# Keys on both partition halves by transposes in place of a DMA, and a new order of activation functions in a decoder layer

## The chip, the cores and the metric

The kernel runs on one core of a Trainium2 chip. The metric is the device time of one launch in microseconds (us), the median of several runs. Lower is better.

## The reference

The program is one decoder layer on a sequence of 256 tokens with 2048 features, all in float32. The part that matters here is the mixer in the middle: one product of the normalised input with a wide weight `w_in` gives queries, keys, values, the inputs of an RWKV-7 recurrence, and gates.

```python
x = x + 0.5 * swiglu(rms_norm(x, ffn1_norm), ...)
h = rms_norm(x, mix_norm); p = h @ w_in
q, k, v, p_rwkv, gates = split(p)
# 16 query heads of 64, 4 key/value heads, window 128, one sink logit for each head
s = where(valid, q k^T / 8, -1e30); m = max(max(s), sink)
e = exp(s - m); pr = e / (sum(e) + exp(sink - m)); y_attn = pr v
# RWKV-7: decay and rate from small products, then a scan over time
w_log = -softplus(-(w0 + tanh(xw) @ w2)) - 0.5      # decay = exp(-exp(w_log))
a = sigmoid(a0 + xa @ a2);  g = sigmoid(xg) @ g2
x = x + (sigmoid(g1) * (y_attn @ w_proj_attn) + sigmoid(g2) * (y_rwkv @ w_proj_rwkv)) @ w_out
x = x + cross_attention(x, mem); x = x + 0.5 * swiglu(rms_norm(x, ffn2_norm), ...)
return rms_norm(x, final_norm)
```

## The kernel before

TensorE (PE) does all matrix products, and nearly all of its time goes to products with weights that are read once from HBM. To keep float32 accuracy, every weight and every activation is split into a high part and a low part, and each product is three matmuls: high x high (line 412), high x low weight (413), low activation x high (414). ScalarE (ACT) casts a weight tile to its high part (line 339), VectorE (DVE) subtracts it from the raw tile to get the low part (line 340). `product` goes over the rows of a weight in items of two 128-row blocks. In the mixer one item is twelve matmuls: six for each half of the tokens. Two items ahead of the one in use are split in advance, and there are three buffers each for high and low parts.

All other work is written as Python generators ("steps") that are put into groups with `bg.spawn`. `product` calls `bg.tick()` after each half item (six matmuls), and at each tick the generators move on by one `yield`. So the interleaving of small work with products is fixed when the program is built. `idle(n)` lets n ticks pass, and `wait_for(name)` yields until another generator has added the name to `bg.seen`. Within that order a scheduler of the language decides the final order on each engine, and `tc.issue_after(ins)` adds an edge that holds an instruction behind `ins` in its engine's queue.

The edited part is the start of the mixer, in this order of products: queries (two products), keys and values (one), then the 288 "small" columns of RWKV, then RWKV keys (two), gates, and so on.

- Keys and values: `scaled` evicts the product to `tok_kv` with the norm's factor (line 783). `keys_values` transposes the 256 key columns on PE (`feat`, line 600), and two ACT copies (line 810) bring the heads to a layout where head kv stands on one half of the partitions. Scores need a key head on both halves, since two query heads share one matmul tile. So the other half is filled by two DMAs from `kd` to `kd`, issued by GpSimd (POOL, line 811). Two DVE copies (line 814) take the values out of `tok_kv`. Three ticks later "kv" is seen.
- Attention: eight generators `attend(kv, qb)`, at most two of them at a time. Scores are matmuls on 64 partitions into score banks of the ring `mm`, which has three (line 831); DVE evicts them with the mask (837), takes the maximum (844) and the negated maximum (849); ACT takes exponentials (856); DVE normalises (864); PE transposes (870) and ACT copies to `pt` (873); PE multiplies with V (878); ACT and DVE split the result (885, 886).
- Decay and rate: `decay_and_rate` waits for the small columns and for the whole attention, then takes a tanh (939) and a sigmoid (940), two small products (950), sixteen sigmoids (957), a scan on DVE (964), and exponentials (978, 982, 983, 985).
- ACT holds the tables of one set of functions at a time. Where the next function is not in it, an ACT_TABLE_LOAD stands ahead of it. In this part, from the first exponential of attention to the last of the decay, there are seven, at lines 856, 940, 856, 957, 978, 957 and 982.

Of the kernel before, what the change touches and what calls it, by code (L numbers as in the profile page):

```python
# [9 lines left out]
AF = mybir.ActivationFunctionType  # L10
# [5 lines left out]
P = 128  # L16
# [7 lines left out]
DECAY = 0.6065306597126334  # L24
# [108 lines left out]
def decoder_layer(ctx: ExitStack, tc: tile.TileContext, a: dict, out: bass.AP):  # L133
# [9 lines left out]
    bg = Interleave()  # L143
# [24 lines left out]
    def idle(n):  # L168
        for _ in range(n):
            yield  # L170
# [596 lines left out]
    with tc.tile_pool(name="mx", bufs=1, reuse_waits="tile") as sp:  # L767
# [12 lines left out]
        def scaled(pb, r, n=512):  # L780
            s = t4("tok", (P, 2, 512))
            for t in range(2):
                act.activation(s[:, t, :n], pb[t][:, :n], AF.Copy, scale=r[t])
            return s
# [11 lines left out]
        for h in range(2):  # L796
            tok = scaled(product(n2.x, W["w_in"]), n2.r)
            qt.append(t4("qt"))
            bg.spawn("feat", to_features(tok, qt[h], "q"))
        tok_kv = scaled(product(n2.x, W["w_in"]), n2.r)  # L800
        kd = t4("kd")
        vt = t4("vt", (P, 2, KV_W))

        def keys_values():

            b = feat(tok_kv, C4[:2])
            v = kd[:].rearrange("p (c e) t -> p c e t", e=2)
            for e in range(2):
                r, o = slice(64 * e, 64 * e + 64), slice(64 - 64 * e, 128 - 64 * e)
                act.copy(v[r, :, e, :], b[r])  # L810
                pool.dma_start(v[o, :, e, :], v[r, :, e, :])
            yield
            for t in range(2):
                dve.tensor_copy(vt[:, t, :], tok_kv[:, t, KV_W : 2 * KV_W])
            yield from idle(3)
            bg.seen.add("kv")

        bg.spawn("feat", keys_values())
        ya = act_tiles("ya", 2)
        sink4 = sinks[:].rearrange("p (k c e) -> p k e c", k=4, c=2)  # L820

        def attend(kv, qb):
            yield from wait_for("kv")
            w = P * (qb + 1)
            tq = slice(qb * P, qb * P + P)
            s = t4("s", (P, 2, 2, T))
            b = [mm() for _ in range(2)]
            for c in range(2):
                for e in range(2):
                    r = slice(64 * e, 64 * e + 64)  # L830
                    pe.matmul(
                        b[e][:, c * w : (c + 1) * w], qt[kv // 2][r, 2 * (kv % 2) + c, tq],
                        kd[r, kv, :w], start=True, stop=True,
                    )
            bias = abias[:, 1 - qb :, :].rearrange("p a b -> p (a b)")
            for e in range(2):
                dve.scalar_tensor_tensor(
                    s[:, e, :, :w], b[e][:, : 2 * w].rearrange("p (c w) -> p c w", c=2), 0.125,
                    bias.unsqueeze(1).to_broadcast([P, 2, w]), ALU.mult, ALU.add,
                )  # L840
            yield
            s3 = s[:].rearrange("p e c w -> p (e c) w")
            m = stat.tile([P, 4], F32, tag="m", name="m")
            dve.tensor_reduce(m[:], s3[:, :, :w], AX.X, ALU.max)
            sk = sink4[:, kv]
            m22 = m[:].rearrange("p (e c) -> p e c", e=2)
            dve.tensor_tensor(m22, m22, sk, ALU.max)
            nm = stat.tile([P, 4], F32, tag="nm", name="nm")
            dve.tensor_scalar(nm[:], m[:], -1.0, None, ALU.mult)
            es = stat.tile([P, 4], F32, tag="es", name="es")  # L850
            dve.tensor_tensor(es[:].rearrange("p (e c) -> p e c", e=2), sk, m22, ALU.subtract)
            yield
            den = stat.tile([P, 4], F32, tag="den", name="den")
            act.activation(es[:], es[:], AF.Exp)
            for i in range(4):
                act.activation(
                    s3[:, i, :w], s3[:, i, :w], AF.Exp, bias=nm[:, i : i + 1],
                    accum_out=den[:, i : i + 1],
                )
            yield  # L860
            dve.tensor_tensor(den[:], den[:], es[:], ALU.add)
            dve.reciprocal(den[:], den[:])
            for i in range(4):
                dve.tensor_scalar(s3[:, i, :w], s3[:, i, :w], den[:, i : i + 1], None, ALU.mult)
            yield
            pt = t4("pt", (P, 2, 4, P))
            for kb in range(qb + 1):
                b = tr()
                for i in range(4):
                    pe.transpose(  # L870
                        b[:, i * P : (i + 1) * P], s3[:, i, kb * P : (kb + 1) * P], ident[:]
                    )
                act.copy(pt[:, kb], b[:].rearrange("p (i q) -> p i q", i=4))
            yield
            b = tr()
            for kb in range(qb + 1):
                for e in range(2):
                    pe.matmul(
                        b[64 * e : 64 * e + 64, : 2 * P], vt[:, kb, kv * 64 : kv * 64 + 64],
                        pt[:, kb, 2 * e : 2 * e + 2, :].rearrange("p c q -> p (c q)"),  # L880
                        start=kb == 0, stop=kb == qb,
                    )
            b3 = b[:, : 2 * P].rearrange("p (c q) -> p c q", c=2)
            hi, lo = (ya.at(p, 2 * kv, 2)[:, :, tq] for p in range(2))
            act.copy(hi, b3)
            dve.tensor_tensor(lo, b3, f32(hi), ALU.subtract)
            if qb:
                ya.done |= {2 * kv, 2 * kv + 1}
            if kv == 3 and qb:
                bg.seen.add("attn")  # L890
# [42 lines left out]
        def decay_and_rate():  # L933
            yield from wait_for("small")
            yield from wait_for("attn")
            wa = t4("wa", (P, RW))
            pool.dma_start(wa[0:64, :], W["rwkv_w2"])
            pool.dma_start(wa[64:128, :], W["rwkv_a2"])
            act.activation(xwa[0:64, :], xwa[0:64, :], AF.Tanh)
            act.activation(xg, xg, AF.Sigmoid)  # L940
            yield
            for h in range(2):
                cs.append(t4("cs"))
                aa.append(t4("aa"))
                for q in (0, 2):
                    b = [mm() for _ in range(2)]
                    for i in range(2):
                        for e in range(2):
                            r, c = slice(64 * e, 64 * e + 64), (4 * h + q + i) * P
                            pe.matmul(  # L950
                                b[e][:, i * T : (i + 1) * T], wa[r, c : c + P], xwa[r, :],
                                start=True, stop=True,
                            )
                    for i in range(2):
                        for e, (dst, bias) in enumerate(((cs[h], w0), (aa[h], a0))):
                            c = 4 * h + q + i
                            act.activation(
                                dst[:, q + i, :], b[e][:, i * T : (i + 1) * T], AF.Sigmoid,
                                bias=bias[:, c : c + 1],
                            )  # L960
                    yield from idle(2)
            for h in range(2):
                for c in range(4):
                    dve.tensor_tensor_scan(
                        cs[h][:, c, :], keep2, cs[h][:, c, :], 0.0, ALU.mult, ALU.add
                    )
                    if c % 2:
                        yield
                c3 = halves(cs[h])
                mid = stat.tile([P, 8], F32, tag="mid", name="mid")  # L970
                dve.tensor_copy(mid[:], c3[:, :, 63])
                dve.tensor_tensor(
                    c3, c3, mid[:].unsqueeze(2).to_broadcast([P, 8, P]), ALU.subtract
                )
                dec.append(stat.tile([P, 4], F32, tag="dec", name="dec"))
                dve.tensor_tensor(dec[h][:], cs[h][:, :, 127], mid[:, 1:8:2], ALU.add)
                yield
                act.activation(dec[h][:], dec[h][:], AF.Exp, scale=-DECAY)

                ee.append(t4("ee", (P, 8, P)))  # L980
                e0.append(stat.tile([P, 8], F32, tag="e0", name="e0"))
                act.activation(e0[h][:], mid[:], AF.Exp, scale=DECAY)
                act.activation(ee[h][:], c3, AF.Exp, scale=-DECAY)
                yield
                act.activation(cs[h][:], cs[h][:], AF.Exp, scale=DECAY)
                yield
            bg.seen.add("decay")
# [526 lines left out]
```

## Time and profile before

| | us |
|---|---|
| median of three runs | 2266.72 |
| lowest and highest of the three | 2265.14, 2268.05 |
| the profiled execution's own time | 2268.04 |
| its span in the profile | 2266.3 |
| PE busy | 2248.0 (99%) |
| DVE busy | 1781.8 (79%) |
| ACT busy | 1232.0 (54%) |
| POOL busy | 134.0 (6%) |

Times in profile rows count from the start of the span. In rows of a timeline the columns are start, duration, engine, line, operation, and in brackets the idle time of the engine ahead of it and what ended that. In rows of stretches they are the stretch, its length, then the busy time and the number of instructions for each engine, the granted clock of PE (1.00 is full speed), the share of DMA time and GB/s. In rows of waits they are the engine and line that waited, what it waited for, the total, the count and the longest. PE's matmuls are pipelined, so that their durations overlap; the distance of their starts is what one costs.

### The profile page before, as it was taken

The page shows a single profiled execution, that of the slowest core. Times are in us where ns is not written, and L with a number is a line of the kernel's source. Part 1 is how long each engine was busy: PE and PEld are TensorE (multiplying, and loading weights), DVE is VectorE, ACT ScalarE, POOL GpSimd, SP SyncE. Part 2 cuts the span into 40 slices and gives each one's busy share as a digit, 9 for nine tenths or more (in the row PEclk, how much of TensorE's full clock was granted, in tenths as well). Part 3 has the DMA queues.
Part 4 walks back from the last instruction along what each step waited for, and adds up shares of the span by engine and source line. Part 5 has one row for each costly group of instructions (what it writes and reads, how often), then busy time and mean ns, then how long its engine had stood idle before and what let it go on. Part 6 is the DMA issues. An engine that isn't in the chain of part 4 may idle for free.

```text
span 2266.3 us, 28104 instructions
## 1 busy us (share of the span) xinstructions
PE 2248.0 (99%) x10613; PEld 1843.9 (81%) x10613; DVE 1781.8 (79%) x2283; ACT 1232.0 (54%) x1655; POOL 134.0 (6%) x194
## 2 busy tenths in 40 slices
PE   9999999999999999999999999999999999999998
PEld 7888888888888877788888888888888888888886
DVE  7899989998988477895444466547899988998987
ACT  6555555555556477544344446456555455555554
POOL 1000000000001000201220030001000000000001
PEclk9999999999999999999999999999999999999999
DMA  7565565565556544677533576657555566556564
GB/s 262 186 208 200 186 215 193 186 209 200 199 197 198 167 122 140 196 231 211 148 87 90 161 260 223 198 165 269 195 193 203 198 204 204 186 201 208 186 205 147
DMA packets 219239, 432.75 MB, mean 191 GB/s; under 512 B 14139, under 2 KB 16416, under 8 KB 219104
## 3 DMA queue, kind: packets, MB, share of 16 engines
q1 hardware_dynamic: 210432, 404.78, 54.3%
q0 software_dynamic: 8208, 25.39, 3.6%
q8 instruction: 83, 1.36, 0.3%
q10 hardware_dynamic: 464, 0.79, 0.1%
q14 instruction: 52, 0.43, 0.1%
HBM read 417.56 MB, written 13.11 MB: 190 GB/s over the span
## 4 chain that ended last, share of the span: by engine, by line
PE 90%; issue 4%; DVE 3%; DMA 1%; ACT 1%; POOL 0%; SPq 0%; POOLq 0%; DVEq 0%; ACTq 0%
PE acc L412 18%; PE acc L413 18%; PE acc L414 18%; PE mm L413 8%; PE mm L414 8%; PE mm L412 8%; PE tr L600 2%; PE tr L413 2%; PE tr L414 2%; PE tr L412 2%; PE mm L1213 1%; DVE lo L340 1%; PE tr L1182 1%; DVE x L573 0%; DMA raw<-in_w_out_dram 0%
## 5 line engine op out<-in xcount | busy, mean ns | idle before, releaser
L340 DVE TENSOR_TENSOR lo<-raw,hi 128x1024 fp32r<-128x1024 f32 (+1 forms) x770 | 895.6, 1165 | 346.3 <-ACT hi L339 344.4
L339 ACT CAST hi<-raw 128x1024 fp32r<-128x1024 f32 (+1 forms) x770 | 759.7, 997 | 737.2 <-PE acc L414 511.5
L412 PE MATMUL acc<-hi,xhi 128*128 128x512 f32 (+1 forms) x1196 | 477.8, 400 | 1.8 <-ACT xhi L627 1.8
L413 PE MATMUL acc<-lo,xhi 128*128 128x512 f32 (+1 forms) x1196 | 466.5, 390 | 1.6 <-DVE lo L340 1.6
L414 PE MATMUL acc<-hi,xlo 128*128 128x512 f32 (+1 forms) x1196 | 465.6, 390 | 0.0
L412 PEld LDWEIGHTS acc<-hi,xhi 128*128 128x128 f32 x1196 | 225.7, 189 | 51.3 <-issue 5.4
L413 PEld LDWEIGHTS acc<-lo,xhi 128*128 128x128 f32 x1196 | 225.9, 189 | 48.9 <-DVE lo L340 3.4
L414 PEld LDWEIGHTS acc<-hi,xlo 128*128 128x128 f32 x1196 | 225.3, 188 | 47.5 <-DVE xlo L628 1.0
L347 ACT CAST thi<-raw 128x1024 fp32r<-128x1024 f32 x172 | 179.0, 1051 | 62.2 <-DVE raw L368 48.8
L348 DVE TENSOR_TENSOR tlo<-raw,thi 128x1024 fp32r<-128x1024 f32 x172 | 208.5, 1221 | 0.7 <-ACT thi L347 0.4
L412 PE MATMUL mm<-hi,xhi 128*128 128x512 f32 x380 | 149.3, 393 | 0.0
L414 PE MATMUL mm<-hi,xlo 128*128 128x512 f32 x380 | 148.1, 390 | 0.0
L413 PE MATMUL mm<-lo,xhi 128*128 128x512 f32 x380 | 148.1, 390 | 0.0
L413 PE MATMUL acc<-lo,hhi 128*128 128x512 f32 x372 | 145.5, 391 | 0.8 <-DVE lo L340 0.8
L414 PE MATMUL acc<-hi,hlo 128*128 128x512 f32 x372 | 145.5, 391 | 0.0
L412 PE MATMUL acc<-hi,hhi 128*128 128x512 f32 x372 | 144.9, 390 | 0.0
L414 PEld LDWEIGHTS mm<-hi,xlo 128*128 128x128 f32 x380 | 71.3, 188 | 15.0
L412 PEld LDWEIGHTS mm<-hi,xhi 128*128 128x128 f32 x380 | 71.4, 188 | 14.5
L413 PEld LDWEIGHTS mm<-lo,xhi 128*128 128x128 f32 x380 | 71.4, 188 | 14.5
L413 PEld LDWEIGHTS acc<-lo,hhi 128*128 128x128 f32 x372 | 69.8, 188 | 15.5 <-DVE lo L340 1.2
L412 PEld LDWEIGHTS acc<-hi,hhi 128*128 128x128 f32 x372 | 69.8, 188 | 14.4
L414 PEld LDWEIGHTS acc<-hi,hlo 128*128 128x128 f32 x372 | 69.9, 188 | 13.9
(386 smaller groups left out, 3551.6 us busy)
## 6 DMA issues: line engine op xcount, KB each, us to landing
raw<-in_ffn_w_up_dram SPq DMA_DIRECT2D x88, 1024.0 KB, 5.5
raw<-in_ffn_w_down_dram SPq DMA_DIRECT2D x88, 1024.0 KB, 5.2
raw<-in_ffn_w_gate_dram SPq DMA_DIRECT2D x84, 1024.0 KB, 5.2
raw<-in_w_in_dram SPq DMA_DIRECT2D x136, 512.0 KB, 3.8
raw<-in_w_out_dram SPq DMA_DIRECT2D x32, 512.0 KB, 4.5
raw<-in_w_proj_attn_dram SPq DMA_DIRECT2D x16, 512.0 KB, 3.7
raw<-in_w_proj_rwkv_dram SPq DMA_DIRECT2D x16, 512.0 KB, 6.1
raw<-in_w_cross_kv_dram SPq DMA_DIRECT2D x16, 512.0 KB, 4.0
```

Source lines behind the costliest of these rows:

```text
L339: at["hi"] = act.copy(hi[:, s], raw[:, s])
L340: at["lo"] = dve.tensor_tensor(lo[:, s], raw[:, s], f32(hi[:, s]), ALU.subtract)
L347: act.copy(hi[:], v[:])
L348: dve.tensor_tensor(lo[:], v[:], f32(hi[:]), ALU.subtract)
L412: pe.matmul(o, xh, hi, start=first, stop=False, **how)
L413: pe.matmul(o, xh, lo, start=False, stop=False, **how)
L414: pe.matmul(o, xl, hi, start=False, stop=last, **how)
L600: pe.transpose(b[:, o : o + P], tok[:, t, col : col + P], ident[:])
L1182: pe.matmul(b[e][:, m * P : (m + 1) * P], x1[r, j, cs_], x2[r, j, cs_], start=True, stop=True,)
L1213: pe.matmul(vb[:, o : o + P][:, r], lhs(e), rhs[:, r], start=first and e == 0, stop=True, **ek,)
```

## The change

The heads of the keys are evicted twice, side by side: one ACT activation for each half of the tokens reads each 64-column key head two times from PSUM and writes a tile of 512 columns, and a second one evicts the values straight into `vt`. The generator that already serves the queries, `to_features`, then transposes four blocks of 128 columns (eight transposes, two copies) into `kd`, so that each head stands on both halves of the partitions. The DMAs, the DVE copies and the pause of three ticks go. In `attend`, two plain yields become `idle(2)`, and the last exponential is remembered. The tanh and the first sigmoid are held behind that exponential, and the decay's exponentials behind the last of the sixteen sigmoids. In the built program, the table loads in this part are then three, ahead of the first attention exponential, the first sigmoid (940 before) and the first decay exponential (978 before). Numbers of lines after this part are lower by three to four in the changed kernel.

```diff
-        tok_kv = scaled(product(n2.x, W["w_in"]), n2.r)
+
         kd = t4("kd")
         vt = t4("vt", (P, 2, KV_W))
-
-        def keys_values():
-
-            b = feat(tok_kv, C4[:2])
-            v = kd[:].rearrange("p (c e) t -> p c e t", e=2)
-            for e in range(2):
-                r, o = slice(64 * e, 64 * e + 64), slice(64 - 64 * e, 128 - 64 * e)
-                act.copy(v[r, :, e, :], b[r])
-                pool.dma_start(v[o, :, e, :], v[r, :, e, :])
-            yield
-            for t in range(2):
-                dve.tensor_copy(vt[:, t, :], tok_kv[:, t, KV_W : 2 * KV_W])
-            yield from idle(3)
-            bg.seen.add("kv")
-
-        bg.spawn("feat", keys_values())
+        pb = product(n2.x, W["w_in"])
+        tok = t4("tok", (P, 2, 512))
+        for t in range(2):
+            act.activation(
+                tok[:, t, :].rearrange("p (h e d) -> p h e d", h=4, e=2),
+                pb[t][:, :KV_W].rearrange("p (h d) -> p h d", h=4).unsqueeze(2).to_broadcast(
+                    [P, 4, 2, 64]
+                ),
+                AF.Copy, scale=n2.r[t],
+            )
+            act.activation(vt[:, t, :], pb[t][:, KV_W : 2 * KV_W], AF.Copy, scale=n2.r[t])
+        bg.spawn("feat", to_features(tok, kd, "kv"))
...
             for i in range(4):
-                act.activation(
+                at["exp"] = act.activation(
                     s3[:, i, :w], s3[:, i, :w], AF.Exp, bias=nm[:, i : i + 1],
...
                 dve.tensor_scalar(s3[:, i, :w], s3[:, i, :w], den[:, i : i + 1], None, ALU.mult)
-            yield
+            yield from idle(2)
             pt = t4("pt", (P, 2, 4, P))
...
                 act.copy(pt[:, kb], b[:].rearrange("p (i q) -> p i q", i=4))
-            yield
+            yield from idle(2)
             b = tr()
...
-            act.activation(xwa[0:64, :], xwa[0:64, :], AF.Tanh)
-            act.activation(xg, xg, AF.Sigmoid)
+            with tc.issue_after(at["exp"].ins):
+                act.activation(xwa[0:64, :], xwa[0:64, :], AF.Tanh)
+                act.activation(xg, xg, AF.Sigmoid)
...
-                            act.activation(
+                            sigmoid = act.activation(
                                 dst[:, q + i, :], b[e][:, i * T : (i + 1) * T], AF.Sigmoid,
...
-                act.activation(dec[h][:], dec[h][:], AF.Exp, scale=-DECAY)
+                with tc.issue_after(sigmoid.ins):
+                    act.activation(dec[h][:], dec[h][:], AF.Exp, scale=-DECAY)
...
-                act.activation(e0[h][:], mid[:], AF.Exp, scale=DECAY)
-                act.activation(ee[h][:], c3, AF.Exp, scale=-DECAY)
+                with tc.issue_after(sigmoid.ins):
+                    act.activation(e0[h][:], mid[:], AF.Exp, scale=DECAY)
+                    act.activation(ee[h][:], c3, AF.Exp, scale=-DECAY)
```

## The prediction, made before the changed kernel ran

> **What bounds the kernel now.** I read the page's first part, then the waits of TensorE (PE) between 784 and 900 us, where the edited code runs, then stretches of that part.
>
> ```profile
> span 2266.3 us, 28104 instructions
> PE 2248.0 (99%) x10613; PEld 1843.9 (81%) x10613; DVE 1781.8 (79%) x2283; ACT 1232.0 (54%) x1655; POOL 134.0 (6%) x194
> ```
> ```profile
> core 0: us, PE busy (x) PEld busy (x) DVE busy (x) ACT busy (x) POOL busy (x), PEclk, DMA share, GB/s
> 784.00:811.00 27.00, 25.50 (x159) 21.41 (x158) 16.87 (x41) 14.96 (x35) 1.27 (x2) 0.87 0.48 141
> 811.00:823.00 12.00, 10.98 (x63) 7.03 (x61) 8.90 (x27) 8.44 (x27) 0.00 (x0) 1.00 0.30 88
> 823.00:840.00 17.00, 16.72 (x86) 12.01 (x85) 13.61 (x33) 13.27 (x33) 3.81 (x6) 1.00 0.52 141
> 840.00:855.00 15.00, 14.69 (x73) 10.67 (x73) 10.86 (x27) 10.93 (x29) 0.00 (x0) 1.00 0.39 119
> 855.00:875.00 20.00, 17.79 (x85) 12.12 (x84) 14.06 (x21) 17.24 (x31) 3.05 (x4) 1.00 0.20 57
> 875.00:910.00 35.00, 35.00 (x156) 28.21 (x156) 27.38 (x27) 25.21 (x33) 2.28 (x4) 1.00 0.64 194
> ```
>
> PE is busy 2248.0 of 2266.3 us, so this change can only win idle PE or a slow PE clock. The stretches are the first pair of attention blocks (784 to 811), the other three pairs, the decay (855 to 875) and what follows. PE idles 1.50, 1.02, 0.28, 0.31 and 2.21 us in them, 5.32 in all, then nothing: from 875 to 910 it is busy 35.00 of 35.00. The only clock below 1.00 is in the first. Idle PE in these stretches and that slow clock are all there is to win.
>
> ```profile
> PE acc L413 <- DVE lo L340: 1.6, 2, 1.3
> PE mm L831 <- DMA kd<-kd: 1.3, 1, 1.3
> PE mm L950 <- ACT cs L957: 0.9, 1, 0.9
> PE tr L870 <- DVE s L864: 0.7, 2, 0.5
> PE tr L878 <- ACT pt L873: 0.6, 1, 0.6
> ```
>
> Each row has the total, the count and the longest. The change touches the causes of all five.
>
> **Keys without the DMA.** PE reaches the first scores (L831) while the keys' DMA, issued by POOL at 786.59, is under way:
>
> ```profile
> 786.59 1.27 POOL L811 DMA_DIRECT2D kd<-kd  x2 [55.50 <-ACT kd L810]
> 790.61 0.93 PE L831 MATMUL mm<-kd,qt 64*128 64x128 f32 x8 [1.33 <-DMA kd<-kd]
> 791.71 2.07 PE L831 MATMUL mm<-kd,qt 64*128 64x256 f32 x6 [0.17 <-DVE s L837]
> ```
> ```profile
> 788.25:791.66 3.41, 1.96 (x15) 1.20 (x13) 1.33 (x4) 0.53 (x1) 0.00 (x0) 1.00 0.92 251
> 791.66:798.49 6.83, 6.78 (x26) 5.96 (x27) 4.77 (x12) 2.90 (x8) 0.00 (x0) 0.50 0.24 70
> 870.17:873.58 3.41, 2.12 (x10) 1.24 (x8) 3.31 (x5) 3.39 (x5) 0.00 (x0) 1.00 0.15 58
> ```
>
> The wait costs 1.33 us. Then the granted clock is 0.50 for 6.83 us, with PE busy in nearly all of them: 6.83 x 0.5 = 3.4 us of work lost, more than the wait itself. Ahead of the drop PE was busy 1.96 of 3.41 us (57%); I took half of 6.83 as the length to compare. A stretch as long, on the same grid, with 2.12 busy (62%) kept its clock at 870. So I read a threshold near 60% of 3.41 us, crossed here because of the DMA wait. [...]
>
> What replaces the DMA: the built order has four more transposes (eight for four), and the first scores wait for the first of two copies into kd only.
>
> ```profile
> 784.98 0.70 PE L600 MATMUL tr<-ident,tok 128*128 128x128 f32 x4
> 785.43 0.38 PE L412 MATMUL acc<-hi,xhi 128*128 128x288 f32 x1
> 787.24 0.29 PE L413 MATMUL acc<-lo,xhi 128*128 128x288 f32 x1
> 787.37 0.29 PE L414 MATMUL acc<-hi,xlo 128*128 128x288 f32 x1
> 785.71 1.19 ACT L810 COPY kd<-tr 64x512 f32<-64x512 f32 x2
> 786.34 0.49 DVE L814 COPY vt<-tok 128x256 f32<-128x256 f32 x2
> ```
>
> Four transposes hold PE from 784.98 to 785.43: +0.45. Two copies into kd stay two (0.6 each, now all 128 partitions). DVE loses two copies of vt (0.49 together); ACT gains two evictions of 256 columns, 0.5 each by the sigmoid rows below, bounds 0.3 to 0.7. They stand ahead of the first kd copy, which then ends near 786.8. PE needs it at 787.6, since its 288-column items and four transposes lie between. So they cost nothing here; with the cover gone, 0.8 us at most. POOL loses two DMAs, for which nothing else queued.
>
> Scores now start one item (12 matmuls) earlier in PE's order, with less product work between them and the softmax:
>
> ```profile
> 796.25 1.28 ACT L856 ACT_TABLE_LOAD   x1
> 797.54 0.40 ACT L856 ACTIVATE s<-s,nm 128x128 f32<-128x128 f32 x1
> 801.26 0.65 ACT L339 CAST hi<-raw 128x576 fp32r<-128x576 f32 x1
> 800.82 1.57 PE L831 MATMUL mm<-kd,qt 64*128 64x128 f32 x12
> 801.80 1.14 DVE L864 TENSOR_SCALAR s<-s,den 128x256 f32<-128x256 f32 x4
> ```
>
> Before, 7.5 us pass from the end of the scores (791.71 + 2.07 = 793.78) to the end of the exponentials (801.26), and 1.7 more to normalised scores (801.80 + 1.14 = 802.94). PE, at half clock, had work all that time. After: scores near 787.7 to 790.7; exponentials end 7.5 later, at 798.2; normalised at 799.9. PE's work between is 42 short matmuls, 0.13 apart (787.24 and 787.37) = 5.6, then 1.5 of the next scores and 0.5 of transposes: it arrives at 798.4. The cast of the next weights stands behind the exponentials in ACT's order, so it lands at 798.9, and its low half, behind the normalising on DVE, at 800.6. I count +1.2 of new idle: 0.4 for the cast and 0.8 in transposes and low half. Bounds: 0 (if PE arrives later) and 2.0.
>
> First pair: -1.33 - 3.4 + 0.45 + 1.2 = -3.1 us.
>
> **Two pauses for one in the attention steps.** Before the transposes and before the product with V, each pair now lets two half items pass, not one. The 0.6 (pt) and 0.7 (s) waits above should shrink. Against it, the fourth pair issues all its scores in a row with three score banks, so the fourth waits for the first's eviction (0.17 above), and everything behind it. I take 0, bounds -1.6 (all idle from 811 to 855: 1.02 + 0.28 + 0.31) and +1.5 (as much new).
>
> **Fewer table loads.** Seven loads stand in this part before; three remain in the built order, since the sigmoids now follow all the exponentials, and the decay's exponentials follow all sigmoids.
>
> ```profile
> L957 ACT ACTIVATE aa<-mm,rv 128x256 f32<-128x256 f32 x8 | 3.8, 493 | 1.5 <-PE mm L950 1.5
> ```
> ```profile
> 867.39 0.39 PE L412 MATMUL acc<-hi,xhi 128*128 128x512 f32 x1
> 867.62 0.40 PE L413 MATMUL acc<-lo,xhi 128*128 128x512 f32 x1
> 867.67 1.28 ACT L957 ACT_TABLE_LOAD   x1
> 869.34 0.47 ACT L957 ACTIVATE aa<-mm,rv 128x256 f32<-128x256 f32 x1
> 869.70 0.48 ACT L957 ACTIVATE cs<-mm,rv 128x256 f32<-128x256 f32 x1
> 870.41 2.01 ACT L339 CAST hi<-raw 128x1024 fp32r<-128x1024 f32 x2
> 872.28 2.35 DVE L340 TENSOR_TENSOR lo<-raw,hi 128x1024 fp32r<-128x1024 f32 x2
> 873.55 0.50 PE L413 MATMUL acc<-lo,xhi 128*128 128x512 f32 x1 [1.29 <-DVE lo L340]
> ```
>
> Four loads less are 4 x 1.28 = 5.1 us of ACT. That is no PE time except where ACT ends a wait: from 855 to 875, where ACT is busy 17.24 of 20. There loads and sigmoids push a weight cast to 870.41, its low half follows at 872.28, and PE waits 1.29. In the built order one cast now stands behind each four sigmoids, and the groups of decay matmuls (L950) are 12 product matmuls apart, 12 x 0.23 = 2.8 us by the two PE rows' starts. Sigmoids start 0.36 apart (869.34, 869.70) and a cast takes 1.0 (2.01 for two), so ACT needs 4 x 0.36 + 1.0 = 2.4 and keeps up. So the 0.92 wait for a bank (the L950 row above, 0.9) goes too. I take -2.1 of the 2.21 idle, bounds -2.2 and 0. Tanh and sigmoid are held behind the last exponential; behind them ACT has casts and copies for attention's end, and the work waiting for tanh (L950) comes 12 matmuls later, so I cost the wait at 0. Past this, the RWKV chain runs 36 product matmuls later in PE's order and ends 102 ahead of its first user, so 0, bounds -0.5 and +1.
>
> **Sum.** -3.1 + 0 - 2.1 = -5.2 us on the profiled execution, whose own time was 2268.04 us (span plus 1.7): 2262.8. Its time is 1.3 above the median of the three runs, 2266.72. I cannot tell whether the profiled one is slower as such or whether the clock drop comes in some runs only (the three spread from 2265.14 to 2268.05). I take half of it off: 2262.1, which is 0.2% under the median.
>
> **The rivals.**
> [...]
> - *The decay keeps its waits* (0.09): the casts come late behind sigmoids and PE waits for lo as before. Time 2262.1 + 2.1 = 2264.2.
> - *A clean run* (0.10): no idle left from 784 to 875. -5.32 - 3.4 + 0.45 = -8.3, so about 2268.0 - 8.3 - 0.65 = 2259.1.
> - *Slower* (0.07): the half clock comes once in each pair, since each now queues scores, bank wait and softmax wait densely. It decides once PE is busy under about 60% of 3.41 us in each of four pairs, as 57% did once before. Then 4 x 3.4 = 13.6 on top: 2275.7, 0.4% slower than 2266.72.
>
> **How the numbers follow.** My forecast has 0.60, and its own range is 2260 to 2264.5. 0.2% (4.5 us, about what a measurement of this kernel can tell from no change) puts the mark at 2262.2, inside it: I give 0.36 of the 0.60 to faster, 0.24 to within. With the clean run faster is 0.46; with the first two rivals within is 0.47; slower is 0.07. The range leaves out the slower rival and the edges: 2258.6 (the clean run, half a microsecond lower) to 2266.5 (2265.5 and one more for the pairs).
>
> **What would show it.** Right: no slow clock near 790; no DMA into kd; first scores with a wait of 0.5 or less; PE idle from 784 to 811 near 1.2; three table loads; PE idle from 855 to 875 under 0.5. Wrong: a clock of 0.50 anywhere in the attention; PE idle over 2 us in the first or the last pair; a PE wait for lo behind the sigmoids; more than 1 us of idle past 900.

## The result, and the profile after

The changed kernel takes 2262.53 us (median of 16 runs, 2262.00 to 2263.34); the kernel before, run beside it, 2266.15 (median of 16, 2264.81 to 2268.45). The ratio is 0.9985, with a 95% interval from 0.9978 to 0.9992: 3.6 us or 0.15% faster. The forecast was 2262.1, "faster" and "within 0.2%" nearly even. So the time came out as forecast; the experiments show that most of its terms did not.

The head of the page after, and the stretches of the edited part (columns as before):

```profile
span 2261.6 us, 28110 instructions
PE 2246.8 (99%) x10617; PEld 1845.5 (82%) x10617; DVE 1778.4 (79%) x2281; ACT 1226.9 (54%) x1653; POOL 132.2 (6%) x192
```
```profile
784.00:811.00 27.00, 26.84 (x181) 22.17 (x179) 19.87 (x50) 18.78 (x51) 0.00 (x0) 1.00 0.43 133
811.00:823.00 12.00, 10.96 (x60) 6.87 (x59) 7.72 (x24) 8.12 (x26) 1.14 (x2) 1.00 0.26 87
823.00:840.00 17.00, 16.92 (x91) 12.47 (x90) 14.01 (x37) 9.80 (x22) 1.84 (x4) 1.00 0.61 185
840.00:855.00 15.00, 15.00 (x80) 10.62 (x79) 8.75 (x20) 13.75 (x36) 2.00 (x3) 1.00 0.34 107
855.00:875.00 20.00, 20.00 (x97) 15.19 (x96) 15.22 (x22) 15.10 (x28) 0.28 (x2) 1.00 0.43 131
```

PE's idle time is now 0.16, 1.04, 0.08, 0 and 0 us, where it was 1.50, 1.02, 0.28, 0.31 and 2.21. The clock is 1.00 throughout. The waits of PE from 784 to 900 us are down to three:

```profile
PE tr L600 <- ACT tok L783: 0.8, 1, 0.8
PE tr L600 <- DVE yalo L882: 0.3, 1, 0.3
PE mm L827 <- DVE s L833: 0.2, 1, 0.2
```

Three table loads are left, as the built order had said (1.28 us each, as before, where the last six stood at the turns between exponentials and sigmoids, 832.48 to 872.44 us):

```profile
791.99 1.28 ACT L852 ACT_TABLE_LOAD   x1
848.26 1.28 ACT L937 ACT_TABLE_LOAD   x1
868.10 1.28 ACT L976 ACT_TABLE_LOAD   x1
```

The end of the first pair's scores, and the cast that stands behind its exponentials:

```profile
789.15 1.13 PE L827 MATMUL mm<-kd,qt 64*128 64x256 f32 x6 [0.16 <-DVE s L833]
797.00 0.66 ACT L339 CAST hi<-raw 128x576 fp32r<-128x576 f32 x1
```

Stretches cut by the clock hold different work in the two kernels. A fairer cut is by PE's product matmuls (lines 412 to 414), of which both kernels have the same 8958: from the 3301st to the 3421st (first pair), to the 3523rd (other pairs), the 3619th (decay), the 4195th (up to the RWKV chain) and the 4963rd (the chain). The length in each row is then the time of the same product work. First before, then after:

```profile
778.75:810.93 32.18, 30.68 (x181) 25.69 (x180) 18.31 (x43) 17.01 (x38) 1.27 (x2) 0.89 0.47 137
810.93:851.30 40.37, 39.02 (x202) 27.77 (x201) 30.75 (x83) 30.03 (x82) 3.81 (x6) 1.00 0.41 118
851.30:885.83 34.53, 32.05 (x155) 23.07 (x154) 21.64 (x29) 30.37 (x51) 3.05 (x4) 1.00 0.43 124
885.83:1027.64 141.81, 141.50 (x656) 114.42 (x654) 126.19 (x161) 67.79 (x73) 20.46 (x19) 1.00 0.69 211
1027.64:1311.41 283.77, 283.36 (x1665) 235.41 (x1664) 135.93 (x162) 127.13 (x230) 43.41 (x69) 1.00 0.48 137
```
```profile
778.96:807.55 28.59, 28.43 (x186) 23.79 (x184) 18.02 (x42) 17.64 (x40) 0.00 (x0) 1.00 0.41 126
807.55:846.96 39.41, 38.29 (x202) 27.57 (x201) 30.72 (x83) 28.14 (x81) 2.98 (x6) 1.00 0.43 134
846.96:877.78 30.82, 30.82 (x154) 22.45 (x152) 19.22 (x28) 24.00 (x42) 2.28 (x4) 1.00 0.46 143
877.78:1019.81 142.03, 141.27 (x655) 114.21 (x653) 117.83 (x154) 71.05 (x79) 21.05 (x17) 1.00 0.65 206
1019.81:1306.51 286.70, 286.29 (x1665) 238.18 (x1665) 142.16 (x169) 126.74 (x230) 45.09 (x70) 1.00 0.44 138
```

Differences: -3.6, -1.0, -3.7, +0.2 and **+2.9**; with +0.2 ahead and +0.2 behind, the span's -4.7 (the medians stand 3.6 apart). By kind and number the small matmuls in each stretch are the same in both kernels, but for the four more transposes in the first. The last row is the surprise. PE is busy in all but 0.4 us in both, at a clock of 1.00, with 896 small matmul records in both traces, and still needs 2.9 us more.

### The profile page after: what moved, and what is told of

The parts are those of the page before. It is cut to its first block, busy times and chain, and to the rows that moved or that the text cites. A ratio compares the mean times of both kernels' runs of the same rounds, so it can differ in the third digit from the quotient of the medians.

```text
span 2261.6 us, 28110 instructions
## 1 busy us (share of the span) xinstructions
PE 2246.8 (99%) x10617; PEld 1845.5 (82%) x10617; DVE 1778.4 (79%) x2281; ACT 1226.9 (54%) x1653; POOL 132.2 (6%) x192
## 4 chain that ended last, share of the span: by engine, by line
PE 96%; DVE 2%; issue 1%; DMA 1%; ACT 1%; SPq 0%; POOL 0%; POOLq 0%; DVEq 0%; ACTq 0%
PE acc L412 19%; PE acc L413 19%; PE acc L414 19%; PE mm L414 8%; PE mm L412 8%; PE mm L413 8%; PE tr L600 2%; PE tr L413 2%; PE tr L412 2%; PE tr L414 2%; PE mm L1212 1%; PE tr L1181 1%; DVE lo L340 1%; DMA raw<-in_w_out_dram 0%; PE mm L827 0%
```

## The experiments

Each kernel ran beside the kernel before. "Alternating" below is said of the score matmuls of the RWKV chain (line 1182 before, 1181 after): two heads, one on each half of the rows, three matmuls each. The program writes them in turn. In the built order 8 of the 16 blocks keep that order before and 5 after; 6 and 8 have three of one head ahead of three of the other, the rest is mixed. (The expectations below speak of three such blocks in the changed kernel and six with the keys alone; the traces have five and seven, in a few of which the pairs start 13 ns apart and not 6 to 7.) I take it that the scheduler's choice depends on when the score banks come free, which no run tests.

**Keys alone.** The keys' part of the diff on the kernel before, nothing else:

```diff
-        tok_kv = scaled(product(n2.x, W["w_in"]), n2.r)
...
-        bg.spawn("feat", keys_values())
+        pb = product(n2.x, W["w_in"])
...
+        bg.spawn("feat", to_features(tok, kd, "kv"))
```

> The kernel before with the keys' part of the change alone (double eviction, eight transposes, no DMA, no pause of three ticks); the pauses in attention and the order of the functions stay as before. My theory: the DMA wait of 1.33 us was the cause of the half clock, so both go: -1.33 - 3.4 + 0.45 for four more transposes = -4.3 us by the end of the attention; the seven table loads and the 2.2 us of idle from 855 to 875 stay. The RWKV chain stands 12 product matmuls earlier, with 6 of its blocks of score matmuls alternating between the row halves where before has 8, for about +1.3. Sum -3.0 us. Rival: the half clock has another cause and stays: -1.33 + 0.45 + 1.3 = +0.4 us.

Measured: 2265.69 us (2265.39 to 2266.97), ratio 0.9997 (0.9988 to 1.0006): no difference that can be told. No half clock (1.00 from 784 to 811 us) and no DMA wait, as expected, and the first pair takes 29.67 us for 32.18, though 76 small matmuls now fall into this stretch for 60. But the chain's stretch takes 285.49 us, 1.7 more than before, and of the waits near the decay the one for cs grows from 0.9 us, the one for lo stays:

```profile
PE mm L946 <- ACT cs L953: 1.4, 2, 1.1
PE acc L413 <- DVE lo L340: 1.3, 1, 1.3
```

Both theories were off at the median: it stands 0.9 us below the runs beside it, not 3.0 below and not 0.4 above.

**Function order and pauses alone**, with the keys by DMA as before:

```diff
-            yield
+            yield from idle(2)
...
+            with tc.issue_after(at["exp"].ins):
...
+                with tc.issue_after(sigmoid.ins):
```

> The kernel before with the order of the functions and the pauses of two ticks, but the keys by DMA as before. My theory: the 1.33 us wait and the half clock (3.4 us) stay; the decay wins 3.7 us as in the whole change, the later pairs of attention about 1; the RWKV chain stands 48 product matmuls later with 3 alternating blocks of score matmuls for 8, for about +3.5. Sum -1.2 us. Rival: table loads are no time of TensorE at all and the gain near the decay came from the keys: +3.5 us.

Measured: 2271.14 us (2269.40 to 2277.36), ratio 1.0026 (1.0015 to 1.0036). Slower than either theory had it. The wait for the keys' DMA is there, as expected (1.6 us for 1.33); the half clock, also expected, did not come in the profiled execution (1.00 from 784 to 811 us). The decay is without waits, but the work behind it falls late among the products. From 870 to 1030 us PE waits 2.4 us for a cast, 1.2 for a bank of `lt` and 0.5 for a low half; the stretch ahead of the chain takes 147.4 us for 141.8, the chain 288.0.

**Scores two ticks later**, the DMA kept:

```diff
-            yield from idle(3)
+            yield from idle(5)
             bg.seen.add("kv")
```

> The kernel before with the keys' pause five ticks instead of three: the DMA stays, but the first scores come 12 short matmuls (12 x 0.13 = 1.6 us) later, so that it has landed. My theory: the wait alone made the half clock, so 1.33 + 3.4 go, at most 1 us of new idle comes, and the chain's order (6 alternating blocks for 8, 4 half ones for 1) costs 0.7: -3.0 to -4.0 us. Rival: the clock falls for another reason than this wait (the matmuls on half the rows, the DMA traffic): the half clock stays and the time changes by -1.3 + 0.7 = -0.6 us.

Measured: 2261.03 us (2260.36 to 2261.58), ratio 0.9976 (0.9967 to 0.9985): 5.6 us faster, more than the 3 to 4 that my theory had, and the best of all kernels here. One number in the program beats the whole change by 1.5 us. The wait is gone and the clock stays at 1.00; the first pair takes 26.9 us, with 56 small matmuls in the stretch for 60. The decay's wait for lo falls from 1.3 to 0.5 us although all seven table loads are still there. That work, too, moved against the products; I take this to be the reason.

**The chain shifted alone.** Six ticks, 36 product matmuls, ahead of the mark that the decay is done:

```diff
+            yield from idle(6)
             bg.seen.add("decay")
```

> The kernel before with six ticks of pause (36 product matmuls) ahead of the mark that the decay is done, so that the RWKV chain has the place and the order of the changed kernel; nothing else is edited. My theory: attention and decay as before, half clock included; the stretch of the chain takes 3.0 us more for the same matmuls, since 3 of the score blocks alternate between the row halves where before has 8; whole time +3.0 us. Rival: the order of the small matmuls is indifferent and the lost 3 us came from elsewhere in the change: 0 us, within 0.5.

Measured: 2268.68 us (2268.04 to 2271.19), ratio 1.0011 (1.0002 to 1.0020). Three stretches of this kernel: the first pair, 3.41 us with the DMA wait in them, and the chain:

```profile
778.71:808.22 29.51, 27.88 (x182) 23.11 (x181) 17.86 (x43) 17.01 (x38) 1.28 (x2) 1.00 0.49 149
787.24:790.65 3.41, 2.07 (x16) 1.71 (x15) 1.52 (x2) 0.99 (x2) 0.59 (x1) 1.00 0.85 218
1025.11:1311.82 286.71, 286.30 (x1664) 238.06 (x1665) 142.16 (x169) 126.69 (x230) 44.95 (x70) 1.00 0.45 138
```

The chain takes 286.71 us, the changed kernel's 286.70 to a hundredth, and PE's matmuls stand in the same order in both: the shift alone makes the 2.9 us. And something nobody had asked: up to the decay this program has the same order as the kernel before, and waits the same 1.3 us for the DMA, yet in this execution the clock did not fall. The same 120 products took 29.51 us in place of 32.18. So the half clock comes in some executions only, and the 6.83 us of it cost 2.7 us.

**Alternation forced, in the changed kernel:**

```diff
+                one = None
...
-                        pe.matmul(
+                        with tc.issue_after(one.ins) if one else nullcontext():
+                            one = pe.matmul(
```

> The changed kernel, with the six score matmuls of each RWKV block held in the order of the code (each behind the one before), so that they alternate between the two halves of the rows; in the built order 3 blocks alternate wholly as before and 13 are one matmul, a little product work, then five that alternate, in place of 3, 4 and 3 by 3. My theory: the order of the halves sets the time of these matmuls; at 0.87 us for an alternating block and about 1.15 for one and five, 21.6 us of this line become 17.6: -4.0 us against the changed kernel, 2258.5. Rival: the order only shows which bank came free late, and TensorE waits that time out instead: 0, 2262.5.

Measured: 2262.64 us (2262.40 to 2263.21), where the changed kernel has 2262.53: nothing. The chain takes 286.8 us. By the distances of the starts the score matmuls did become cheaper, by 2.0 us, but the first of each block now stands apart, product work is broken into 83 times for 71, and the products around took 1.9 us more. 14 blocks became one and five, 2 alternate wholly. So the edit made a new cost where it took one away; it tells nothing against the alternation, and nothing for it.

**The same edit in the kernel before.**

> The same edit in the kernel before, where 8 blocks alternate already and 8 become one and five. My theory: 19.4 us of this line become 16.2: -3.2 us against before, and the stretch of the RWKV chain is then about 1.4 us shorter than in the changed kernel with the same edit, not 2.9. Rival: waits take the place of the order: 0.

Measured: 2266.51 us (2264.94 to 2268.12), ratio 1.0001 (0.9992 to 1.0010). The chain takes 283.11 us for 283.77. Of the 3.2 us expected 0.7 came. By the starts the score matmuls take 2.2 us less, but product work takes 1.3 more (85 breaks for 77).

**Three by three, in the kernel before.** Exchanging the loops was to take the alternation away; it adds no break:

```diff
-                for m, (x1, x2) in enumerate(((kh, ah), (kh, rh), (bh, rh))):
-                    for e, r in enumerate(rows):
+                for e, r in enumerate(rows):
+                    for m, (x1, x2) in enumerate(((kh, ah), (kh, rh), (bh, rh))):
```

> The kernel before with the two loops around the RWKV score matmuls exchanged: three of one half of the rows, then three of the other; nothing else. 8 blocks that alternated (0.87 us) become three by three (1.59). My theory: the alternation is worth 0.72 us in each of the 8: the stretch of the chain goes from 283.8 to 289.6 us, and the whole time up by 5.8 to 2272. Rival: the price by starts is only moved between neighbours, as in the run that forced the alternation in the changed kernel: the stretch stays within 1 us of 283.8.

Measured: 2269.72 us (2268.08 to 2272.74), ratio 1.0015 (1.0006 to 1.0024). The chain takes 286.39 us, 2.6 more. But the eight blocks did not become three by three. In the trace the two heads are staggered, so that the second head's first matmul starts 6 ns behind the first head's second. The first rows of such a block, and the product matmul behind it:

```profile
1106.82 0.49 PE L1182 MATMUL tr<-at,aa 64*128 64x128 f32 x2
1107.14 0.27 PE L1182 MATMUL tr<-rt,aa 64*128 64x128 f32 x1
1107.15 0.37 PE L1182 MATMUL tr<-at,aa 64*128 64x128 f32 x1
1107.26 0.27 PE L1182 MATMUL tr<-rt,aa 64*128 64x128 f32 x1
```
```profile
1108.01 0.50 PE L412 MATMUL acc<-hi,xhi 128*128 128x512 f32 x1
```

It takes 1108.01 - 1106.82 = 1.19 us for 0.87, and 8 x 0.32 = 2.6 us. By the starts all 16 blocks take 3.2 us more, while 0.4 us of waiting and 0.1 us of product work go. So the chain pays most of what the starts say, against the rival; the 0.72 us between alternating and three by three was not put to the test.

**Three by three, in the changed kernel.**

> The same exchange in the changed kernel, where only 3 blocks alternate wholly and 3 partly. My theory: 3 x 0.72 + 3 x 0.3 = 3.1 us on the stretch, 286.7 to 289.8, so that both kernels have the same stretch when both run three by three; whole time 2265.6. Rival: the 2.9 us between the two kernels lie elsewhere than in the alternation, and the stretches stay 2.9 apart (both move by the same, or not at all).

Measured: 2263.30 us (2262.99 to 2263.78); the chain 287.69 us, 1.0 more. Here, too, the five alternating blocks became staggered ones of 1.19 us: 1.6 us more by the starts, with 0.4 us of waiting and 0.2 us of product work gone. The chains' stretches in the two kernels with the loops exchanged:

```profile
1028.20:1314.59 286.39, 286.39 (x1666) 238.66 (x1664) 135.85 (x162) 127.03 (x230) 43.42 (x69) 1.00 0.44 136
```
```profile
1019.69:1307.38 287.69, 287.69 (x1665) 240.06 (x1665) 142.16 (x169) 126.68 (x230) 45.08 (x70) 1.00 0.44 137
```

They stand 1.3 us apart, not 2.9 and not 0. That does not split the 2.9 us, since the exchange did not make the two alike: the first has eight staggered blocks, one mixed and seven three by three, the second five, three and eight, and by the starts their score matmuls still differ by 0.7 us. What can be counted is this: from the kernel before to the changed one the score matmuls take 2.3 us more by the starts (21.6 for 19.4), the other small matmuls 1.4 more, product work 0.7 less, and waiting is the same. This is an account, not a test of each part. That it is the order, whatever else differs, is borne out across kernels: the three with one and the same order of matmuls in this stretch (keys alone, no pauses, scores sooner) have 285.49, 285.48 and 285.51 us, the two that share another (later scores, without and with the function order) 284.37 and 284.40.

Here is a block that alternates, in the kernel before, and one that is three by three in the changed kernel (starts and lengths; x4 is both heads in turn, x2 is one head):

```profile
1106.26 0.49 PE L1182 MATMUL tr<-at,aa 64*128 64x128 f32 x4
1106.59 0.39 PE L1182 MATMUL tr<-rt,aa 64*128 64x128 f32 x4
1106.81 0.39 PE L1182 MATMUL tr<-rt,kk 64*128 64x128 f32 x4
1107.13 0.50 PE L412 MATMUL acc<-hi,xhi 128*128 128x512 f32 x1
```
```profile
1138.15 0.48 PE L1181 MATMUL tr<-at,aa 64*128 64x128 f32 x2
1138.48 0.38 PE L1181 MATMUL tr<-rt,aa 64*128 64x128 f32 x2
1138.70 0.39 PE L1181 MATMUL tr<-rt,kk 64*128 64x128 f32 x2
1138.91 0.48 PE L1181 MATMUL tr<-at,aa 64*128 64x128 f32 x2
1139.23 0.38 PE L1181 MATMUL tr<-rt,aa 64*128 64x128 f32 x2
1139.45 0.38 PE L1181 MATMUL tr<-rt,kk 64*128 64x128 f32 x2
1139.77 0.50 PE L412 MATMUL acc<-hi,xhi 128*128 128x512 f32 x1
```

The same twelve records take 1107.13 - 1106.26 = 0.87 us in turn, and 1139.77 - 1138.15 = 1.62 one head after the other.

**Keys by DMA with five ticks, with the function order and the pauses.**

```diff
-            yield from idle(3)
+            yield from idle(5)
             bg.seen.add("kv")
...
+            yield from idle(2)
...
+            with tc.issue_after(at["exp"].ins):
```

> The changed kernel's pauses and function order with the keys by DMA and the pause of five ticks ahead of the scores. My theory: the transposes are not needed, only the wait must go; attention and decay win as in the changed kernel, but the chain of small work stands 12 product matmuls later still than with the DMA and three ticks, where 5 us went in waits past 900 us; so the wait (1.6 us) goes, the chain's order wins 1.5, and the late work stays dear: 2268. Rival: what was lost past 900 us came of the DMA wait itself, and this is then as fast as the changed kernel: 2262.5.

Measured: 2263.64 us (2262.12 to 2267.29), ratio 0.9988 (0.9979 to 0.9997), 4.4 us below my theory and 1.1 above the rival. The DMA hidden is nearly as good as the transposes. The profiled execution, 2267.29, shows a new wait, 1.8 us for the DMA of the decay's weights (line 951 waits for `wa`), and a clock of 0.50 for 3.41 us behind it (859.23 to 862.64).

**The change without its pauses.**

```diff
-            yield from idle(2)
+            yield
```

> The changed kernel with plain yields in attention in place of the pauses of two ticks: keys by transposes and function order alone. My theory: the gain of the decay (3.7 us) belongs to the function order, so this is the keys-only kernel (2265.7) less 3.7: 2262.0, with the chain's order (6 alternating blocks) better than in the changed kernel but the later pairs' idle of about 1 us back. Rival: the decay's gain came from the pauses, which shift it: 2265.7.

Measured: 2262.26 us (2261.92 to 2263.64), ratio 0.9981 (0.9972 to 0.9989); 2262.0 was expected. The function order on top of the keys is worth 2265.69 - 2262.26 = 3.4 us. Its waits of PE from 784 to 900 us have neither cs nor lo in them:

```profile
PE tr L874 <- ACT pt L869: 0.6, 1, 0.6
PE mm L827 <- DVE s L833: 0.2, 1, 0.2
```

The pauses give nothing: 2262.26 without them, 2262.53 with them. In the traces the span is 1.0 us shorter without them: the chain, which then has the order of the keys alone, takes 285.48 us for 286.70, while the three stretches up to the end of the decay take 99.6 us for 98.8.

**Later scores and the function order**, plain yields, keys by DMA:

```diff
-            yield from idle(3)
+            yield from idle(5)
             bg.seen.add("kv")
...
+            with tc.issue_after(at["exp"].ins):
```

> The kernel before with five ticks in place of three ahead of the scores (as the run with the later scores, 2261.0) and the function order of the change; keys by DMA, plain yields in attention. My theory: the two gains add where they do not share a wait; the later scores left 0.5 for lo and 0.4 for cs near the decay, so the function order can win 1 us more: 2260.0. Rival: the function order wins its own 3.4 us, as it did on top of the keys by transposes (2265.7 to 2262.3): 2257.6.

Measured: 2262.92 us (2262.57 to 2264.20), ratio 0.9986 (0.9977 to 0.9995). It is 1.9 us slower than with later scores alone, against both theories. The first pair and the chain have the same order as there and nearly the same times (26.8 us for 26.9, 284.4 in both); the 1.9 us lie in the other pairs and the decay, where casts are late at other places now:

```profile
PE acc L413 <- DVE lo L340: 1.7, 2, 1.0
PE tr L878 <- ACT pt L873: 0.9, 1, 0.9
PE tr L600 <- ACT tok L783: 0.6, 1, 0.6
```

So the function order was worth -3.4 us on one placement and +1.9 on another.

**Scores two ticks sooner.**

```diff
-            yield from idle(3)
+            yield from idle(1)
             bg.seen.add("kv")
```

> The kernel before with one tick in place of three ahead of the scores, so that TensorE waits some 1.6 us longer for the keys' DMA, 2.9 in all. My theory: with 1.33 us the half clock came in some executions and not in others; with 2.9 us of idle TensorE is busy under 60% of whatever 3.41 us hold it, so the half clock comes in each: +1.6 wait, 2.8 us of half clock in every run where before had it in some (+1.6 at the median), +1.3 for the chain's order: +4.5 us, 2271, with the runs closer together than those of before (2264.6 to 2269.4). [...]

Measured: 2267.91 us (2267.32 to 2269.62), ratio 1.0010 (1.0001 to 1.0019). The time is 3 us under my theory's 2271, but the test failed: the wait did not grow. The scheduler moved only the scores that need no DMA (787.54); those behind it still run at 791.02, after a wait of 1.25 us. No half clock came there (1.00 from 784 to 811 us). One came at 862.0 in the decay (a mean clock of 0.75 over 6.83 us), behind a wait of 1.3 us for a bank of line 950 (two such waits take 1.6 us there).

## Why the prediction was right, and where it was not

The total held by luck: errors of opposite sign met. Of -5.2 us forecast for the profiled execution the traces show -4.7. The first three stretches gave 0.5, 1.0 and 1.6 us more than the sum had, the RWKV chain took 2.9 back, and 0.6 went elsewhere. By the terms of the sum:

- *First pair, -3.1; measured -3.6.* The DMA wait (-1.33) went. The half clock costs 2.7, not the 3.4 that 6.83 x 0.5 gives: this is the pair of rows 32.18 and 29.51 above. The four transposes cost some 0.35 (by their starts), for 0.45. The new idle of 1.2 did not come: PE idles 0.16 us here. That step failed; it let the cast and the low half land behind PE's arrival, and they did not. The 7.5 us from the scores to the end of the exponentials were carried over, but they took 6.7 (789.15 + 1.13 to 797.00): the exponentials ended at 797.0 and not at 798.2, the cast at 797.7 and not at 798.9, and PE came to its next product matmul at 798.8.
- *The half clock as a loss of every run.* I left it open whether the drop comes in some runs only, and took half of 1.3 us off. It does come in some only: the kernel with the chain shifted has the wait without the drop. The runs say the same. Kernels with the DMA wait at three ticks spread over 3.2 to 8.0 us (before 3.6, chain shifted 3.2, function order 8.0), the kernels without that wait and without a new DMA wait (changed, keys alone, later scores, no pauses) over 1.2 to 1.7. And of the 95 executions of the kernel before that ran beside the experiments, those with a mean granted clock of 0.999 have a median of 2265.3 us, those with 0.998 2266.4, those with 0.997 2267.7. So the profile of before, one with the drop, showed more to win than the median had. At the median the keys alone are worth 0.9 us: the drop that they remove comes in some runs only, and they lose 1.7 us in the chain.
- *A threshold near 60% of 3.41 us.* Refuted: 1.84 us busy of 3.41 (54%) had no drop behind it, 2.21 (65%) had one; see the last section.
- *Pairs two to four, 0; measured -1.0.* PE's idle falls from 1.35 to 1.12 us. The rest is small work that costs less: by starts, 56 small matmul records take 8.05 us for 8.62, and 36 transposes 3.93 for 4.20. The sum took the price of a small matmul as fixed; by these starts it changes with the place in the order.
- *Decay, -2.1; measured -3.7.* The mechanism is shown on this placement: with the function order the waits for cs and lo go (keys alone against no pauses). The term was too small. The stretch's 2.48 us of idle went whole (34.53 - 32.05 before, 30.82 of 30.82 busy after); of the other 1.2, by the starts, 0.8 are the 56 small matmuls (7.7 for 8.5) and 0.4 product work; why they cost less is not shown.
- *RWKV chain, 0 with bounds -0.5 and +1; measured +2.9.* The step that failed outright. I asked who waits for the chain (nobody, 102 matmuls ahead of its user) and not what its matmuls cost where they now stand. The kernel with the chain shifted shows that the new order alone costs the 2.9 us. By the starts the score matmuls, of whose blocks five alternate and not eight, take 2.3 us more, the other small matmuls 1.4, and product work gives 0.7 back; what each part is worth alone stays open.
- *Pauses, 0:* right at the median (+0.3 by the runs), as a gain of 0.8 us up to the end of the decay and a loss of 1.2 in the chain nearly cancel.

The rivals: the half clock, given 0.14 to stay or move (2262.1 + 3.4 = 2265.5), was gone, not moved; the decay lost its waits; no slower mechanism decided. The clean run was nearly reached from 784 to 875 us (1.28 us of idle left), but its time not, for the chain's 2.9 us.

## What to carry to other kernels

On an engine that is 99% busy, moving work is not free because no one waits (here the chain's new place cost 2.9 us): compare the time of equal amounts of the main work, stretch by stretch, and look at stretches where the busy time itself grew. Before replacing a late DMA, try to consume it later: here two more ticks won 5.6 us and the rewrite 3.6. A gain from one placement of interleaved work need not hold on another (the function order: -3.4 us and +1.9), so measure parts together, not only one by one. And look in the trace whether an edit made the order that it was meant to make: the exchanged loops gave staggered blocks, and the scores two ticks sooner left the wait as it was.

## What the runs showed of the hardware

*The half clock.* The clock stood at 0.50 for 6.83 us in before and for 3.41 us with the DMA and five ticks (859.23 to 862.64). So here are stretches of 3.41 us, a length of my choosing, each laid whole steps of 3.41 us from a drop in the same execution: first two without a drop behind them (both of function order alone), then three with one (three by three in before, a mean clock of 0.75 over the 6.83 us behind it; DMA with five ticks; scores sooner, 0.75 over 6.83 us too):

```profile
790.00:793.41 3.41, 2.34 (x16) 1.56 (x17) 1.85 (x4) 0.00 (x0) 0.00 (x0) 1.00 0.78 236
977.74:981.15 3.41, 1.84 (x7) 1.23 (x8) 2.35 (x4) 2.89 (x4) 0.00 (x0) 1.00 0.27 90
```
```profile
790.12:793.53 3.41, 2.21 (x15) 1.43 (x16) 1.73 (x4) 0.00 (x0) 0.00 (x0) 1.00 0.82 234
```
```profile
855.82:859.23 3.41, 1.64 (x7) 0.92 (x6) 1.23 (x1) 0.34 (x2) 0.00 (x0) 1.00 0.97 230
```
```profile
858.59:862.00 3.41, 2.09 (x10) 1.23 (x9) 1.39 (x2) 3.40 (x8) 0.00 (x0) 1.00 0.00 0
```

The stretch of the chain shifted, 787.24 to 790.65, is shown above with 2.07 busy and had no drop behind it either. The clock stayed after 1.84 us of busy PE (54%) and fell after 2.21 (65%), so the busy share alone does not decide. Nor does the longest gap: ahead of the four drops (that of before among them) it was 1.3 to 1.8 us, and gaps of 1.3, 1.6 and 1.7 us in the three stretches without a drop brought none. In all four stretches with a drop half or more of PE's busy time is matmuls on 64 rows (1.41 of 1.96 us, 2.06 of 2.21, 1.33 of 1.64, 1.13 of 2.09), and the 54% one has matmuls on 128 rows alone; but the first row here has 2.06 of 2.34 us such matmuls and no drop, so that this share alone does not decide either. What makes the drop stays open. The same order and the same wait gave a drop in the execution of before and none in that of the chain shifted. The stretch of 3.41 us begins 2.4 us ahead of the end of the wait in the first (788.25, 790.61) and 3.3 ahead of it in the second (787.24, 790.58); whether that made the difference no run tests. The one drop of 3.41 us behind this wait (three by three in before, the same order) cost some 1.4 us: 30.94 us for the 120 products where the chain shifted has 29.51.

*Matmuls on half the rows.* In turn on the two halves they start in pairs 6 to 7 ns apart, as in the block of 0.87 us above; in the block of 1.62 us each start on the same half is 111 to 213 ns behind the last. With the loops exchanged, eight blocks of 0.87 us became 1.19, 2.6 us by the starts, and the whole chain took 2.6 us more.
